# Second layer: half of the gated units as pairs of seven block products, with weight places taken in turn

## The chip, the cores and the metric

The kernel runs on one core of one Trainium2 chip. The metric is the device time of one execution in microseconds. Times given for a kernel are the median of several executions; a profile comes from one more execution, whose own time is given beside it.

## What is computed

One step of a two-layer decoder trunk for 512 prompt positions and 8 sample rows, which share all weights. The kernel treats them as one activation of 520 rows, held as 8 tiles of 128 channels x 520 columns. Only the second layer matters here:

```
def c_mixer(x, w_in, w_s, b_s, norm_v_g, norm_v_b, w_out):
    z = jnp.einsum('bld,de->ble', x, w_in)          # 1024 -> 3 x 2048
    u, v, g = jnp.split(z, (D_C, 2 * D_C), axis=-1)
    u = jax.nn.gelu(u)
    v = layer_norm(jax.nn.gelu(v), norm_v_g, norm_v_b)
    ...
    w_causal = w_s * jnp.tril(jnp.ones((CHUNK, CHUNK), w_s.dtype))
    mix = jnp.einsum('hts,bnshd->bnthd', w_causal, vc) + jnp.transpose(b_s)[None, None, :, :, None]
    ...
    y = u * mix * jax.nn.silu(g)
    return jnp.einsum('ble,ed->bld', y, w_out), v
...
xp = layer_norm(DEEPNORM_ALPHA * xp + out_p, ln_g[l], ln_b[l])
```

The first layer has the same shape: a wide input projection, two convolution branches, a gate, an output projection and a layer norm.

## The kernel before, in words

All matrix work is done in *units*: one unit is a 128-column slice of a weight matrix, 1024 x 128, which the host lays out as a tile of 128 x 8 x 128. There are 136 units; units 0 and 1 have a path of their own at the start. A unit is loaded as float32 (`raw_`), then split into a rounded part `whi_` (a cast on ACT) and the rest `wlo_` (a subtraction on DVE, or for 46 units of the first layer a copy on ACT and an accumulating DMA from POOL). The activations are split in the same way (`xh`, `xl`; `x1h`, `x1l` in the second layer; `yh`, `yl` for what enters an output projection). A product is then three matmuls for each of 8 k-tiles: high x high, low x high, high x low. `mm2` (line 161) does this for both halves of 260 columns, 48 matmuls a unit; `mm` (line 145) for one half, 24 matmuls. The results of a unit lie in a PSUM tile of two banks (`zt`, two such tiles); `cps` and `mps` give two single banks each.

`unit(n)` hands out unit n and loads units up to five ahead (`LEAD`). Weight tiles come from a common pool of 12 (tag W); units 70, 71, 134 and 135 take theirs from a pool M of 4. There are 3 raw tiles, 7 tiles for passing results (T), 4 more (B), and 8 + 8 long-lived tiles (AB and SB).

The code is written as a plain sequence; each instruction's place on its engine is set by a planner ahead of the run, which takes the earliest instruction in the code that can start by its estimated times, raised by `soon()` and lowered by `background()`. Each engine then runs its list strictly in that order and waits on semaphores.

The second layer runs in this order:

- 16 v units: GELU on ACT, then `v_tok` transposes the tile on PE (4 transposes of 128 x 128), copies it to a long-lived tile `vtok`, and takes its statistics on DVE. All 16 `vtok` tiles stay in the on-chip memory.
- `c_group(0)`: four u units (`z_u`, GELU), with `v_finish` after the first, which normalizes all 16 `vtok` tiles on DVE (line 658, 64 instructions). Then four gate units (`z_gc`, SiLU). `mix_unit` makes the mix of one unit from `vtok` (line 713, four matmuls) and `split_y` makes `yh` and `yl`. Then `c_group(4)` in the same way.
- eight output units over the first half of y (`z_q`); their results, with alpha times x1 added, stay in the on-chip memory as `r1`.
- `c_group(8)`, `c_group(12)`, and eight output units over the second half of y (`z_p`, by `out_part`, first columns 0 to 259, then the rest), with the final layer norm.

Of the kernel before, what the change touches and what calls it, by code (L numbers as in the profile page):

```python
# [16 lines left out]
P = 128  # L17
# [24 lines left out]

LEAD = 5
CUT = 260
# [5 lines left out]
def decoder_kernel(  # L50
# [35 lines left out]

    def ab_slot(name):
        return slots.tile([P, T], F32, tag="AB", name=name, bufs=8)

    def tmp(name):  # L90
        return tpool.tile([P, T], F32, tag="T", name=name, bufs=7)

# [18 lines left out]

    n_units = 2 + wu.shape[0]
    units = [None, None]

    def load_unit(wtag=("W", 12)):
        n = len(units)
        raw = wpool.tile([P, KT, P], F32, tag="raw", name=f"raw_{n}", bufs=3)
        nc.sync.dma_start(raw, wu[n - 2])
        hi = wpool.tile([P, KT, P], F32R, tag=wtag[0], name=f"whi_{n}", bufs=wtag[1])
        nc.scalar.copy(hi, raw)  # L120
        lo = wpool.tile([P, KT, P], F32R, tag=wtag[0], name=f"wlo_{n}", bufs=wtag[1])
        if n in BY_DMA:

            nc.scalar.mul(lo, raw, -1.0)  # L124
            nc.gpsimd.dma_start(lo, wu[n - 2], accum_op=ALU.add)  # L125
        else:
            nc.vector.tensor_tensor(lo, raw, hi.bitcast(F32), op=ALU.subtract)  # L127
        units.append((hi, lo))


    BY_DMA = set(range(10, 50)) | set(range(72, 78))
    EXTRA = set()
    for base in (64, 128):
        EXTRA.update((base + 6, base + 7))

    def unit(n):
        while len(units) < min(n + 1 + LEAD, n_units):
            load_unit(("M", 4) if len(units) in EXTRA else ("W", 12))
        return units[n]

# [14 lines left out]

    def mm2(z, w, ah, al):
        hi, lo = w
        for k in range(KT):
            for h in range(2):
                for j, (a, b) in enumerate(((hi, ah), (lo, ah), (hi, al))):  # L160
                    nc.tensor.matmul(  # L161
                        z[h][:, :TH],
                        a[:, k, :],
                        b[k][:, hs(h)],
                        start=(k == 0 and j == 0),
                        stop=(k == KT - 1 and j == 2),
                    )
# [15 lines left out]
    for k in range(KT):  # L183
        x = tmp(f"x_{k}")
        if k % 4 == 0:
            raw = wpool.tile([P, 4, 2, P], F32, tag="raw", name=f"raw_s{k}", bufs=3)
            w0h.append(wpool.tile([P, 4, 2, P], F32R, tag="W", name=f"whi_s{k}", bufs=12))
            w0l.append(wpool.tile([P, 4, 2, P], F32R, tag="W", name=f"wlo_s{k}", bufs=12))
        q, j = k // 4, k % 4
# [28 lines left out]

    load_unit()
    pa = const.tile([P, KT, NPA], F32, name="pa")  # L220
# [13 lines left out]


    unit(1)
    xs = []
    for j in range(2):
        t = wpool.tile([P, 4, NS, WA], F32, tag="M", name=f"xs_{j}", bufs=4)
        nc.sync.dma_start(t, cache_a[:, 4 * j : 4 * j + 4])  # L240
        xs.append(t)
# [45 lines left out]
    for i in range(KT):  # L287
# [24 lines left out]
        nc.gpsimd.dma_start(cap_out[:, i, :], ap[:, SEQ : SEQ + PADA])  # L312
        cA.append(ab_slot(f"cA_{i}"))
        if i % 2 == 1:
# [16 lines left out]
        nc.gpsimd.dma_start(cbp_out[:, i, :], ch[:, SEQ : SEQ + PADB])  # L331
        s = slots.tile([P, T], F32, tag="SB", name=f"sB_{i}", bufs=8)
        sB.append(s)
# [24 lines left out]
    with background():  # L358
        for j in range(2):
            nc.gpsimd.dma_start(cas_out[:, 4 * j : 4 * j + 4], xs[j])  # L360
            proda = wpool.tile([P, 4, NS, WA], F32, tag="M", name=f"proda_{j}", bufs=4)
# [95 lines left out]
    for d in range(KT):  # L457
        xr = tmp(f"xr_{d}")
        nc.sync.dma_start(xr, xT[:, d, :])
        r = slots.tile([P, T], F32, tag="SB", name=f"r_{d}", bufs=8)  # L460
        if d == 2:
# [15 lines left out]
    def out_part(base, c0, c1, yh, yl, res, lnc, done, last=False, pool_sub=()):  # L477
# [39 lines left out]
        def norm():  # L517
# [26 lines left out]
            for d in range(KT):  # L544
# [3 lines left out]
                if last:  # L548
                    if d % 4 == 0:
                        out = wpool.tile([P, 4, nn], F32, tag="raw", name=f"out_{d}", bufs=3)  # L550
                    o = out[:, d % 4, :]
# [39 lines left out]
    vs = tiny.tile([P, NV, NS], F32, name="vs")  # L591
    stats = wpool.tile([P, NC, NV, 6], F32, tag="M", name="stats", bufs=4)

    def v_tok(i):
        nc.gpsimd.tensor_copy(vs[:, i, :], vt[i][:, SEQ:])
        m = mt(f"vt_{i}")
        for c in range(NC):
            nc.tensor.transpose(m[:, c * P : (c + 1) * P], vt[i][:, c * P : (c + 1) * P], ident)  # L598
        t = ab_slot(f"vtok_{i}") if i < 8 else slots.tile([P, T], F32, tag="SB", name=f"vtok_{i}", bufs=8)
        nc.scalar.copy(t[:, :SEQ], m)  # L600
# [10 lines left out]
    for i in range(NVF):  # L611
# [6 lines left out]
        if i > 0:  # L618
            v_tok(i - 1)
    wt = wpool.tile([P, NH, P], F32, tag="M", name="wt", bufs=4)  # L620
    nc.gpsimd.dma_start(wt, wsT_in)
    bs = wpool.tile([P, NH, P], F32, tag="M", name="bs", bufs=4)
    nc.gpsimd.dma_start(bs, bs_in)
# [13 lines left out]
    for i in range(NVF, NV):  # L637
# [3 lines left out]
        nc.scalar.activation(two(vt[i]), zh(z), AF.Gelu_apprx_tanh)  # L641
        v_tok(i - 1)
    n += NV

    mv = tiny.tile([P, NC, 2], F32, name="mv")
    rs = tiny.tile([P, NC], F32, name="rs")
    mixs = tiny.tile([P, NV, NS], F32, name="mixs")
    rowsum = wpool.tile([P, NH, P], F32, tag="M", name="rowsum", bufs=4)

    def v_finish():  # L650
# [4 lines left out]
        nc.gpsimd.tensor_tensor(rs, rs, neg_half[:, :NC], op=ALU.pow)  # L655
        for i in range(NV):
            for c in range(NC):
                nc.vector.tensor_scalar(
                    vtok[i][:, c * P : (c + 1) * P],
                    vtok[i][:, c * P : (c + 1) * P],  # L660
                    mv[:, c, 0:1],
                    rs[:, c : c + 1],
                    op0=ALU.subtract,
                    op1=ALU.mult,
                )

# [37 lines left out]

    def mix_unit(i):
        h = i // 2
# [5 lines left out]
        for c in range(NC):  # L712
            nc.tensor.matmul(  # L713
                m[:, c * P : (c + 1) * P], vtok[i][:, c * P : (c + 1) * P], wt[:, h, :], start=True, stop=True
            )
# [10 lines left out]
        return t  # L726

    def c_group(g0):
        nonlocal n
        gu = []  # L730
        for i in range(g0, g0 + 4):
            z = zt(f"z_u{i}")
            mm2(halves(z), unit(n), x1h, x1l)
            n += 1
            t = btmp(f"gu_{i}")
            nc.scalar.activation(two(t), zh(z), AF.Gelu_apprx_tanh)
            gu.append(t)
            if i == 0:
                v_finish()

        def finish(i):
            t = gu[i - g0]
            split_y(i, t, mix_unit(i), "c", 1)

        for i in range(g0, g0 + 4):
            z = zt(f"z_gc{i}")
            mm2(halves(z), unit(n), x1h, x1l)
            n += 1
            g = tmp(f"silu_c{i}")
            t = gu[i - g0]  # L750
            nc.scalar.activation(two(g), zh(z), AF.Silu)
            nc.vector.tensor_tensor(t, g, t, op=ALU.mult)
            if g0 > 0:
                finish(i)
        if g0 == 0:
            for i in range(4):
                finish(i)

    yh, yl = [], []
    c_group(0)  # L760
    c_group(4)
    res = []
    for d in range(KT):
        z = zt(f"z_q{d}")
        mm2(halves(z), unit(n), yh, yl)
        n += 1
        r = ab_slot(f"r1_{d}")
        nc.vector.scalar_tensor_tensor(
# [3 lines left out]
            r, x1l[d].bitcast(F32), ALPHA, r, op0=ALU.mult, op1=ALU.add  # L772
        )
        res.append(r)
    yh, yl = [], []
    c_group(8)
    c_group(12)

# [108 lines left out]
```

## Time and profile before

| | |
|---|---|
| median of 3 executions | 826.85 us (826.73 to 828.02) |
| the profiled execution's own time | 827.27 us |
| its span, first to last instruction | 825.5 us |
| TensorE matmul busy | 811.8 us, 98% of the span |
| VectorE busy | 527.8 us, 64% |
| ScalarE busy | 351.9 us, 43% |
| GpSimd busy | 90.4 us, 11% |
| moved by DMA | 106.51 MB, 129 GB/s on average |

The times of the engines are busy times, and all engines run at once, so they do not add up. The page also cuts the span into 40 slices and gives each engine's busy share in each slice as a digit in tenths. Groups of instructions are listed by source line as "out<-in xcount | busy us, mean ns of one | idle time before". In the engines' names PE is TensorE, PEld its weight load, DVE VectorE, ACT ScalarE, POOL GpSimd and SP the engine that issues most loads. The v stage runs from about 458 to 520 us (its first part from 420), the gated stages from 520 to 620 and from 666 to 765.

### The profile page before, as it was taken

What the parts mean: (1) busy time and instruction counts of PE and PEld (TensorE: products, weight loads), DVE (VectorE), ACT (ScalarE), POOL (GpSimd) and SP (SyncE); (2) the same over time, 40 slices, a digit from 0 to 9 for tenths busy, and PEclk for the clock granted to TensorE, in tenths of its full rate; (3) what the DMA queues carried; (4) which work ended last, traced back from release to release, by engine and by line L of the source; (5) the groups of instructions that cost most, each with busy time, mean ns of one, the idle gap of its engine ahead of it and who ended that gap; (6) DMA issues with size and microseconds to landing.
All of it is one profiled execution on the core that took longest, in us unless ns stands there. A gap on an engine that the chain in (4) does not pass through costs nothing.

```text
span 825.5 us, 16037 instructions
## 1 busy us (share of the span) xinstructions
PE 811.8 (98%) x6792; PEld 809.9 (98%) x6792; DVE 527.8 (64%) x911; ACT 351.9 (43%) x515; POOL 90.4 (11%) x162
## 2 busy tenths in 40 slices
PE   8999999999999999999999999999999999999994
PEld 8999999999999999999999999999999999999994
DVE  5899998999963477355785423586255333626666
ACT  5544454444454445342668333333332133334243
POOL 0122221222111000000101411000000000000031
PEclk9999999999999999999999999999999999999997
DMA  8698988889878532322472422223322332232011
GB/s 301 203 205 185 215 182 186 184 187 223 180 172 198 180 115 77 104 88 92 113 195 91 163 80 78 77 83 101 100 79 78 102 82 98 77 97 84 1 53 53
DMA packets 33736, 106.51 MB, mean 129 GB/s; under 512 B 4304, under 2 KB 8032, under 8 KB 33664
## 3 DMA queue, kind: packets, MB, share of 16 engines
q1 hardware_dynamic: 26000, 79.01, 31.1%
q0 software_dynamic: 7664, 26.48, 17.0%
q8 instruction: 53, 0.87, 0.4%
q14 instruction: 19, 0.16, 0.1%
HBM read 102.03 MB, written 3.44 MB: 128 GB/s over the span
## 4 chain that ended last, share of the span: by engine, by line
PE 96%; DMA 1%; DVE 1%; ACT 1%; SPq 0%; issue 0%; ACTq 0%; DVEq 0%
PE z_p L145 11%; PE z_gc L161 11%; PE z_u L161 11%; PE z_v L161 7%; PE z_q L161 6%; PE z_o L161 6%; PE z_c L161 6%; PE z_ga L161 6%; PE z_post L161 6%; PE z_h L161 6%; PE z_gb L161 6%; PE z_val L161 5%; PE z_gate L161 5%; PE z_v L145 4%; PE mix L713 2%; PE vt L598 1%
## 5 line engine op out<-in xcount | busy, mean ns | idle before, releaser
L120 ACT CAST whi<-raw 128x1024 fp32r<-128x1024 f32 x134 | 139.9, 1048 | 322.8 <-PE z_u L161 44.9
L127 DVE TENSOR_TENSOR wlo<-raw,whi 128x1024 fp32r<-128x1024 f32 x88 | 107.4, 1225 | 140.5 <-ACT whi L120 140.5
L273 DVE SCALAR_TENSOR_TENSOR acc<-apad,pa,acc 128x512 f32<-128x512 f32 x240 | 165.6, 750 | 3.6 <-ACT acc L270 2.7
L161 PE MATMUL z_gc<-x1h,whi 128*128 128x260 f32 x256 | 72.9, 285 | 0.0
L161 PE MATMUL z_u<-x1h,whi 128*128 128x260 f32 x256 | 72.4, 283 | 0.0
L125 POOL DMA_DIRECT2D wlo<-in_wu x46 | 40.1, 871 | 292.7 <-ACT msq L529 140.3
L161 PE MATMUL z_gc<-x1h,wlo 128*128 128x260 f32 x256 | 72.0, 281 | 0.0
L161 PE MATMUL z_u<-x1l,whi 128*128 128x260 f32 x256 | 72.0, 281 | 0.0
L161 PE MATMUL z_gc<-x1l,whi 128*128 128x260 f32 x256 | 72.0, 281 | 0.0
L161 PE MATMUL z_u<-x1h,wlo 128*128 128x260 f32 x256 | 72.0, 281 | 0.0
L124 ACT ACTIVATE wlo<-raw 128x1024 fp32r<-128x1024 f32 x46 | 48.5, 1055 | 0.0
L161 PEld LDWEIGHTS z_u<-x1h,wlo 128*128 128x128 f32 x256 | 48.1, 188 | 0.1
L161 PEld LDWEIGHTS z_gc<-x1h,wlo 128*128 128x128 f32 x256 | 48.2, 188 | 0.0
L161 PEld LDWEIGHTS z_u<-x1h,whi 128*128 128x128 f32 x256 | 48.1, 188 | 0.1
L161 PEld LDWEIGHTS z_u<-x1l,whi 128*128 128x128 f32 x256 | 48.1, 188 | 0.0
L161 PEld LDWEIGHTS z_gc<-x1l,whi 128*128 128x128 f32 x256 | 48.1, 188 | 0.0
L161 PEld LDWEIGHTS z_gc<-x1h,whi 128*128 128x128 f32 x256 | 48.1, 188 | 0.0
L161 PE MATMUL z_v<-x1h,whi 128*128 128x260 f32 x160 | 46.0, 288 | 0.0
L161 PE MATMUL z_v<-x1l,whi 128*128 128x260 f32 x160 | 45.0, 281 | 0.0
L161 PE MATMUL z_v<-x1h,wlo 128*128 128x260 f32 x160 | 45.0, 281 | 0.0
L161 PE MATMUL z_c<-xh,wlo 128*128 128x260 f32 x128 | 36.1, 282 | 0.3 <-DVE wlo L127 0.3
L145 PE MATMUL z_p<-yh_c,whi 128*128 128x260 f32 x128 | 36.3, 285 | 0.0
(258 smaller groups left out, 2706.0 us busy)
## 6 DMA issues: line engine op xcount, KB each, us to landing
raw<-in_wu SPq DMA_DIRECT2D x134, 512.0 KB, 4.0
wlo<-in_wu POOLq DMA_DIRECT2D x46, 512.0 KB, 7.9
xr<-in_xT SPq DMA_DIRECT2D x8, 260.0 KB, 4.6
x<-in_xT SPq DMA_DIRECT2D x7, 260.0 KB, 4.7
out_y<-r SPq DMA_DIRECT2D x8, 130.0 KB, 1.7
out_y<-out SPq DMA_DIRECT2D x4, 260.0 KB, 2.4
raw_s<-in_w SPq DMA_DIRECT2D x8, 128.0 KB, 4.4
xs<-in_cache_a SPq DMA_DIRECT2D x2, 496.0 KB, 8.5
```

Source lines behind the costliest of these rows:

```text
L120: nc.scalar.copy(hi, raw)
L124: nc.scalar.mul(lo, raw, -1.0)
L125: nc.gpsimd.dma_start(lo, wu[n - 2], accum_op=ALU.add)
L127: nc.vector.tensor_tensor(lo, raw, hi.bitcast(F32), op=ALU.subtract)
L145: nc.tensor.matmul(ps, a[:, k, :], b[k][:, c], start=(k == 0 and j == 0), stop=(k == KT - 1 and j == 2),)
L161: nc.tensor.matmul(z[h][:, :TH], a[:, k, :], b[k][:, hs(h)], start=(k == 0 and j == 0), stop=(k == KT - 1 and j == 2),)
L273: nc.vector.scalar_tensor_tensor(acc[i], apads[i][:, j : j + SEQ], pa[:, i, PA_W + j : PA_W + j + 1], acc[i], op0=ALU.mult, op1=ALU.add,)
L598: nc.tensor.transpose(m[:, c * P : (c + 1) * P], vt[i][:, c * P : (c + 1) * P], ident)
L713: nc.tensor.matmul(m[:, c * P : (c + 1) * P], vtok[i][:, c * P : (c + 1) * P], wt[:, h, :], start=True, stop=True)
```

## The change

In each four of u units and each four of gate units (there are eight fours), the first two units are computed as a pair, as a 2 x 2 block product in the Winograd form of Strassen's scheme. The weight blocks are the two units by the two halves of the 1024 inputs; the activation blocks are the two halves of inputs by the two halves of 260 columns. Seven products of four k-tiles replace eight.

- `load_pair` makes the weight forms of a pair: a11 and a12 (unit 1 as it is), a22, s1, s3, s2 and s4, with four additions on DVE, and each form split into a high and a low part. That is seven weight tiles of full size for a pair.
- `x_forms` makes the four activation forms, during the v units 6, 8, 10 and 12: for each of four k, eight DVE instructions and four casts on ACT, with 260 columns each.
- `Seven` runs the products in the order p1, p5, p2, p6, p7, p4, p3. They accumulate in two PSUM banks (p2 has a third); ACT copies out an intermediate sum and DVE adds others in the on-chip memory. The function then runs on the sum there, not out of PSUM.
- `c_four` puts the third unit of the four between the products: p1, p5, p2, p6, half of unit 3, p7, the other half, p4, p3, then unit 4.
- Weight tiles come from six places of two tiles each, taken in turn; a pair takes four places. Units are loaded ahead until ten tiles are ahead (five single units). The casts of the weights from unit 88 on, and the functions of the fours, are each kept in code order on ACT.
- To make room, each `vtok` tile is stored to memory by a DMA from POOL and fetched again by SP for its mix, with normalizing then (half of it on DVE, half on ACT) in place of line 658; the eight `r1` tiles are stored and fetched too. T has 5 tiles instead of 7, M 3 instead of 4, raw 4 instead of 3.
- In a gate four, the last step of each output (`finish`) comes when its function has run: for the pair and the third unit this is after p3.

```
-LEAD = 5
+RING = 6
+NRAW = 4
+AHEAD = 10
...
+    spill = ctx.enter_context(tc.tile_pool(name="spill", bufs=1, space=bass.MemoryType.DRAM))
...
-        return tpool.tile([P, T], F32, tag="T", name=name, bufs=7)
+        return tpool.tile([P, T], F32, tag="T", name=name, bufs=5)
...
+    def load_pair(n1, n2):
+        r1, r2 = load_raw(n1), load_raw(n2)
+        a1 = parts(n1, r1)
+        a22 = w_slot(f"wa22_{n1}", place_of(), (P, 2, 4, P))
+        high(a22[:, 0], r2[:, 4:], n2)
+        nc.vector.tensor_tensor(a22[:, 1], r2[:, 4:], a22[:, 0].bitcast(F32), op=ALU.subtract)
+        nc.vector.tensor_tensor(r2[:, :4], r2[:, :4], r2[:, 4:], op=ALU.add)
+        nc.vector.tensor_tensor(r1[:, :4], r1[:, :4], r2[:, :4], op=ALU.add)
+        nc.vector.tensor_tensor(r2[:, 4:], r1[:, :4], r2[:, 4:], op=ALU.subtract)
+        s13 = parts(n2, r2, kind="s")
+        nc.vector.tensor_tensor(r1[:, 4:], r1[:, 4:], r1[:, :4], op=ALU.add)
+        s24 = parts(n1, r1, kind="s")
...
+    def need(*job):
+        j = place[job]
+        ahead = lambda: sum(2 if len(q) == 1 else 7 for q in JOBS[j + 1 : len(loaded)])
+        while len(loaded) < len(JOBS) and (len(loaded) <= j or ahead() < AHEAD):
+            q = JOBS[len(loaded)]
+            loaded.append(load_unit(*q) if len(q) == 1 else load_pair(*q))
+        return loaded[j]
...
-        vtok[i] = t
+        vtok[i] = spill.tile([P, SEQ], F32, name=f"vd_{i}")
+        nc.gpsimd.dma_start(vtok[i], t)
...
+        def p1(self):
+            self.w = need(*self.job)
+            z = zt(f"z_{self.key}")
+            self.b1, self.b2 = z[:, 0, :TH], z[:, 1, :TH]
+            product(self.b1, self.w["a11"], self.x(0, 0), True)
+            self.copy(self.c1[:, hs(0)], self.b1)
+        def p5(self):
+            product(self.b2, self.w["s1"], self.f(1), True)
+        def p2(self):
+            b3 = cps.tile([P, SEQ], F32, tag="cv", name=f"z_{self.key}_2")[:, :TH]
+            product(b3, self.w["a12"], self.x(1, 0), True)
+            self.add(self.c1[:, hs(0)], b3)
+        def p6(self):
+            product(self.b1, self.w["s2"], self.f(2))
+            self.copy(self.c1[:, hs(1)], self.b1)
+        def p7(self):
+            product(self.b1, self.w["s3"], self.f(3))
+            self.copy(self.c2[:, hs(1)], self.b1)
+            self.add(self.c2[:, hs(1)], self.b2)
+        def p4(self):
+            product(self.b1, self.w["a22"], self.f(4))
+            self.copy(self.c2[:, hs(0)], self.b1)
+        def p3(self):
+            product(self.b2, self.w["s4"], self.x(1, 1))
+            self.add(self.c1[:, hs(1)], self.b2)
...
+    def fetch(i):
+        t = tpool.tile([P, SEQ], F32, tag="V", name=f"vback_{i}", bufs=2)
+        nc.sync.dma_start(t, vtok[i])
...
+        flight[:] = [Seven(f"{tag}{m}", (m, m + 1), ts[0], ts[1]).steps(), ends]
+        stop()
+        z = zt(f"z_{tag}{m + 2}")
+        w = unit(m + 2)
+        mm2(halves(z), w, x1h, x1l, range(KT // 2))
+        stop()
+        mm2(halves(z), w, x1h, x1l, range(KT // 2, KT))
+        with soon():
+            nc.scalar.copy(two(ts[2]), zh(z))
+        stop(True)
+        apply(2)
+        z = zt(f"z_{tag}{m + 3}")
+        mm2(halves(z), unit(m + 3), x1h, x1l)
+        apply(3, zh(z))
...
+        for e in range(g0, g0 + 4):
+            back[e] = fetch(e)
+        c_four(m + 4, "g", tmp, AF.Silu, lambda j, g: finish(g0 + j, us[j], g))
```

More of the change, by code (lines that the diff above doesn't have):

```diff
@@ L109, in hs, with place_of, w_slot, load_raw @@
         return slice(h * TH, (h + 1) * TH)
[L112 to L117, printed above, removed]
-        nc.sync.dma_start(raw, wu[n - 2])
[L119 to L122, printed above, removed]
+    turn = [0]
+    def place_of():
+        turn[0] += 1
+        return f"W{turn[0] % RING}"
+    def w_slot(name, tag, shape=(P, KT, P)):
+        return wpool.tile(list(shape), F32R, tag=tag, name=name, bufs={"M": 3, "raw": NRAW}.get(tag, 2))
+    def load_raw(n):
+        raw = wpool.tile([P, KT, P], F32, tag="raw", name=f"raw_{n}", bufs=NRAW)
+        nc.sync.dma_start(raw, wu[n - 2])
+        return raw
+    class Chain:
+        def __init__(self):
+            self.last = None
+        def add(self, make):
+            if self.last is None:
+                self.last = make().ins
+            else:
+                with tc.issue_after(self.last):
+                    ins = make().ins
+                self.last = ins
+    casts = Chain()
+    def high(out, src, n):
+        if n >= 88:
+            casts.add(lambda: nc.scalar.copy(out, src))
+        else:
+            nc.scalar.copy(out, src)
+    def parts(n, raw, tags=None, kind="w"):
+        tags = tags or [place_of()] * 2
+        hi = w_slot(f"{kind}hi_{n}", tags[0])
+        high(hi, raw, n)
+        lo = w_slot(f"{kind}lo_{n}", tags[1])
+        if n in BY_DMA and kind == "w":
             nc.scalar.mul(lo, raw, -1.0)
@@ L549, in norm @@
                     if d % 4 == 0:
[L550 removed]
+                        out = wpool.tile([P, 4, nn], F32, tag="raw", name=f"out_{d}", bufs=NRAW)
                     o = out[:, d % 4, :]
@@ new lines, in product, with __init__, x, f @@
+    def product(ps, a, b, first=False):
+        for k in range(4):
+            (ah, al), (bh, bl) = a(k), b(k)
+            for j, (p, q) in enumerate(((ah, bh), (al, bh), (ah, bl))):
+                nc.tensor.matmul(
+                    ps, p, q, start=(first and k == 0 and j == 0), stop=(k == 3 and j == 2),
+                    skip_group_check=True,
+                )
+    class Seven:
+        def __init__(self, key, job, c1, c2):
+            self.key, self.job, self.c1, self.c2 = key, job, c1, c2
+        def x(self, half, h):
+            return lambda k: (x1h[4 * half + k][:, hs(h)], x1l[4 * half + k][:, hs(h)])
+        def f(self, j):
+            return lambda k: (xf[j - 1][k][:, 0], xf[j - 1][k][:, 1])
+        def copy(self, out, src):
+            with soon():
+                nc.scalar.copy(out, src)
+        def add(self, out, src):
+            with soon():
+                nc.vector.tensor_tensor(out, out, src, op=ALU.add)
+        def p1(self):
[23 more added lines that the diff above has]
+            self.add(self.c1[:, hs(1)], self.b2)
+        def steps(self):
+            self.p1()
+            self.p5()
+            self.p2()
+            self.p6()
+            yield
+            self.p7()
+            yield
+            self.p4()
+            self.p3()
@@ L642, in decoder_kernel @@
         v_tok(i - 1)
+        if i % 2 == 0 and i < NVF + 8:
+            x_forms((i - NVF) // 2)
     n += NV
@@ L726, in mix_unit @@
         return t
-    def c_group(g0):
[L729 to L754, printed above, removed]
-        if g0 == 0:
-            for i in range(4):
-                finish(i)
+    back = {}
@@ new lines, in finish, with stop, c_four, apply @@
+    def finish(i, u, g):
+        nc.vector.tensor_tensor(u, u, g, op=ALU.mult)
+        split_y(i, u, mix_unit(i, back[i]), "c", 1)
+    funcs = Chain()
+    flight = [iter(()), lambda: None]
+    def stop(last=False):
+        for _ in flight[0]:
+            if not last:
+                return
+        then, flight[1] = flight[1], lambda: None
+        then()
+    def c_four(m, tag, out, func, done):
+        ts = [out(f"{tag}_{m + j}") for j in range(4)]
+        def apply(j, src=None, sign=1.0):
+            t = ts[j]
+            if src is None:
+                funcs.add(lambda: nc.scalar.activation(t, t, func, scale=sign))
+            else:
+                funcs.add(lambda: nc.scalar.activation(two(t), src, func))
+            done(j, t)
+        def ends():
+            apply(0)
+            apply(1, sign=-1.0)
+        flight[:] = [Seven(f"{tag}{m}", (m, m + 1), ts[0], ts[1]).steps(), ends]
[5 more added lines that the diff above has]
+        mm2(halves(z), w, x1h, x1l, range(KT // 2, KT))
+        with soon():
+            nc.scalar.copy(two(ts[2]), zh(z))
[4 more added lines that the diff above has]
+        apply(3, zh(z))
```

146 lines of the change are left out of this document (98 added, 48 removed).

## The prediction

> **What bounds the kernel now.** I read the page first: span, busy shares, slices, and the shares of the chain that ended last.
>
> ```profile
> span 825.5 us, 16037 instructions
> PE 811.8 (98%) x6792; PEld 809.9 (98%) x6792; DVE 527.8 (64%) x911; ACT 351.9 (43%) x515; POOL 90.4 (11%) x162
> PE   8999999999999999999999999999999999999994
> DVE  5899998999963477355785423586255333626666
> ACT  5544454444454445342668333333332133334243
> PEclk9999999999999999999999999999999999999997
> PE 96%; DMA 1%; DVE 1%; ACT 1%; SPq 0%; issue 0%; ACTq 0%; DVEq 0%
> ```
>
> TensorE (PE) is busy in every slice but the first and the last, at the full granted clock, and is 96% of the chain. A busy PE could still hide waits, so the waits of PE come next, all of them:
>
> ```profile
> PE warm L174 <- DVE warm L171: 1.1, 1, 1.1
> PE z_first L211 <- ACT xh L204: 0.8, 1, 0.8
> PE z_c L161 <- DVE wlo L127: 0.3, 1, 0.3
> ```
>
> They sum to 2.2 us, all at the start. So an instruction taken off PE shortens the run by PE's pitch, as long as nothing new makes PE wait. The pitch is in the chain in order of time (start, us, what, count):
>
> ```profile
> 619.97 46.06 PE z_q L161 x384
> 666.03 22.85 PE z_u L161 x192
> 688.88 5.70 PE z_gc L161 x48
> 695.47 5.73 PE z_gc L161 x48
> 764.72 14.96 PE z_p L145 x125
> ```
>
> 22.85 / 192 = 119.0 ns from one 260-column matmul to the next (a unit of 48 is 5.71 us). Between two z_gc units lie 695.47 − 688.88 − 5.70 = 0.89 us, the four mix matmuls. Then the other engines by stage, since the change works only where u and z_gc are made (520 to 620 and 666 to 765) and in the v stage ahead of it (458 to 520):
>
> ```profile
> core 0: us, PE busy (x) PEld busy (x) DVE busy (x) ACT busy (x) POOL busy (x), PEclk, DMA share, GB/s
> 15.00:189.00 174.00, 173.72 (x1461) 173.52 (x1461) 160.76 (x233) 84.93 (x104) 36.06 (x59) 1.00 0.87 202
> 373.00:458.00 85.00, 85.00 (x710) 84.88 (x709) 56.02 (x138) 52.11 (x102) 11.09 (x14) 1.00 0.45 128
> 458.00:520.00 62.00, 62.00 (x525) 62.00 (x524) 21.11 (x55) 21.08 (x32) 11.52 (x15) 1.00 0.32 95
> 520.00:620.00 100.00, 100.00 (x842) 99.83 (x842) 62.20 (x141) 35.28 (x48) 5.99 (x14) 1.00 0.27 86
> 666.00:689.00 23.00, 23.00 (x196) 23.00 (x195) 6.21 (x6) 7.24 (x9) 0.00 (x0) 1.00 0.30 94
> 689.00:715.00 26.00, 26.00 (x222) 26.00 (x222) 13.51 (x19) 9.88 (x13) 0.75 (x3) 1.00 0.24 82
> 805.00:825.50 20.50, 8.99 (x68) 8.33 (x67) 13.99 (x35) 7.27 (x17) 3.49 (x5) 0.79 0.16 53
> ```
>
> There PE is full, while VectorE (DVE) has 19.7 us of work in a group's 49 us (666 to 715) and ScalarE (ACT) 17.1: room for the additions the change asks of them.
>
> **The change part by part.** Durations of the operations it uses (x count | busy, mean ns | idle):
>
> ```profile
> L120 ACT CAST whi<-raw 128x1024 fp32r<-128x1024 f32 x134 | 139.9, 1048 | 322.8 <-PE z_u L161 44.9 <-PE z_v L161 40.5 <-PE z_q L161 34.5
> L127 DVE TENSOR_TENSOR wlo<-raw,whi 128x1024 fp32r<-128x1024 f32 x88 | 107.4, 1225 | 140.5 <-ACT whi L120 140.5
> L658 DVE TENSOR_SCALAR vtok<-vtok,mv,rs 128x128 f32<-128x128 f32 x64 | 16.5, 347 | 0.4 <-POOL rs L655 0.4
> L491 DVE TENSOR_TENSOR r<-z_p,r 128x260 f32<-128x260 f32 x32 | 13.0, 422 | 12.7 <-PE z_p L145 12.7
> L717 DVE SCALAR_TENSOR_TENSOR mix<-mix,pv,cm 128x512 f32<-128x512 f32 x16 | 12.0, 749 | 29.2 <-PE mix L713 29.2
> L406 DVE TENSOR_TENSOR yl_c<-gu,yh_c 128x520 fp32r<-128x520 f32 x16 | 11.2, 699 | 11.0 <-ACT yh_c L405 11.0
> L752 DVE TENSOR_TENSOR gu<-silu_c,gu 128x520 f32<-128x520 f32 x16 | 11.1, 696 | 0.3
> L404 DVE TENSOR_TENSOR gu<-gu,mix 128x520 f32<-128x520 f32 x16 | 11.1, 694 | 0.2
> L405 ACT CAST yh_c<-gu 128x520 fp32r<-128x520 f32 x16 | 10.0, 627 | 34.8 <-DVE gu L404 34.8
> L736 ACT ACTIVATE gu<-z_u 128x520 f32<-128x520 f32 x16 | 9.6, 601 | 9.4 <-PE z_u L161 9.4
> L708 DVE SCALAR_TENSOR_TENSOR cm<-rowsum,pv,bs 128x128 f32<-128x128 f32 x16 | 5.5, 341 | 0.0
> L751 ACT ACT_TABLE_LOAD x4 | 5.1, 1283 | 0.1
> L610 ACT COPY v<-z_v 128x260 f32<-128x260 f32 x6 | 2.2, 370 | 4.2 <-PE z_v L145 4.2
> ```
>
> *Matmuls.* Two units are 2 x 48 = 96 matmuls; seven products of 4 k-tiles x 3 are 84, with the same 128x128 weights and 260 columns. Eight pairs: 8 x 12 = 96 fewer, 96 x 119.0 ns = **−11.42 us**. No matmul is added: transposes and mix stay. A rule to hold against this: in the Trainium skill's page "TensorE: Matmul & The Clock Gate", section "Wait — 56ns, not 53.3ns?", a warm matmul starts every N / 2.4 GHz plus about 2.5 ns, 110.8 ns for 260 columns, which would make the term 10.64 us. The row says 119.0, and the row is used.
>
> *Handing over PSUM inside a pair.* This wait is new: p6, p7 and p4 write the bank that ACT must first have copied, p3 the one that DVE must have added. Between an emptied product and the next in its bank lie 24 other matmuls (2.86 us; p3: 36, 4.28 us). An ACT copy is 0.37, with one cast ahead of it (1.05) 1.42 us: hidden. The bad case is cast, table load and function first, 1.05 + 1.28 + 0.60 + 0.37 = 3.30, 0.44 late; tables change about once per four, so 8 x 0.44 = 3.5 us is the upper end and 0 the lower (a gain is excluded, PE has no idle to give back here). Nearest row: 373 to 458, where half units of 24 matmuls are emptied by the same engines at some 65% busy, and PE is busy 85.00 of 85 us, though over more banks. I take **+1.0**, near the lower end. If the cover goes, all later matmuls of the four queue behind the waiting one.
>
> *Weight forms.* DVE per pair: three subtractions of 1024 columns (3.68), one of 512 (at most 0.70), four additions of 512 (2.80): 7.2 us where two units had 2.45. Plus three adds from PSUM (1.27) and the two plain units (2.45): 10.9 us per four, against 180 x 0.119 = 21.4 us of PE. A gate four also finishes four outputs, 4 x (0.696 + 0.694 + 0.749 + 0.341 + 0.699) = 12.7, and normalizes four fetched tiles, 8 x 0.347 = 2.8: 26.4 us in 21.4 + 4 x 0.89 = 25.0. The u and gate four together: 37.3 of 46.4 us, 80%. (Means overstate: the group at 666 to 715 would sum to 22.5 by them and shows 19.7.) ACT: 6 casts less one half, four copies, one more copy of a full tile, four functions, half of the normalizing, four casts of y: below 60%. So both fit on average, and the gate four's surplus of 1.4 us is prefetch that can slide. The form due soonest is s24: its place frees after p3, it is needed at the next p6, 48 + 36 matmuls = 10.0 us later; cast and subtraction take 2.3. Cost 0. Without that cover it is 2.3 us per four.
>
> *Six places in turn, raw 4, M 3, T 5.* Still 12 weight tiles, and five units ahead for single units as before. A four uses exactly six places, so a pair's successor waits only for s24 as above. SP is passed by 24 more loads (16 v tiles, 8 residuals), POOL by 24 stores. T from 7 to 5 in the first layer: its reuse is one or two tiles per 5.7 us unit. Cost 0; bounds ±0.5, from the 0.3 + 0.8 us of start waits that one more raw tile can touch.
>
> *v tiles and residual through memory.* 16 x 256 KB and 8 x 260 KB out and back, 12.5 MB over 245 us: 51 GB/s on top of 86, where the first stage carries 202.
>
> ```profile
> raw<-in_wu SPq DMA_DIRECT2D x134, 512.0 KB, 4.0
> wlo<-in_wu POOLq DMA_DIRECT2D x46, 512.0 KB, 7.9
> ```
>
> A store of half that size holds its T tile under 7.9 us, so two of five at one unit per 6.2 us; x_forms takes two for some 4 us: four of five. x_forms on DVE: 4 x 8 x 0.42 = 13.5 us on top of 21.11 in 62 us. The 64 normalizations that ran in one block (16.5 us) are gone from v_finish. All beside PE: 0.
>
> *The ends of the halves.* Silu of three gate units now waits for p3, so four outputs finish together. After p3: silu 0.60, then three chains on DVE of 3 x 3.2 = 9.5 us, then the last unit's. PE meanwhile has m+3 and mix (5.71 + 3.56 = 9.3), then 42 matmuls of z_q (5.0 us) ahead of the last y. The last chain ends about 9.3 + 0.6 + 3.2 + 0.6 = 13.7, cover 14.3. In z_p the cover is shorter, but there, before the change, the last yl_c is this late already:
>
> ```profile
> 769.97 0.70 DVE L406 TENSOR_TENSOR yl_c<-gu,yh_c 128x520 fp32r<-128x520 f32 x1 [0.75 <-ACT yh_c L405]
> ```
>
> It ends 5.9 us after z_p began at 764.72, while 21 matmuls reach the last k in 2.5 us, and PE ran 14.96 us without a wait: it took up later tiles first. Bounds 0 to 2 x 1.5; I take **+0.5**.
>
> **Sum.** The profiled execution took 827.27 us (span 825.5 and 1.8 around it). 827.27 − 11.42 + 1.0 + 0.5 = 817.35. The median shown, 826.85, lies 0.42 lower: **816.9 us**. With every end: 814.9 (no new waits, −0.5) to 822.4 (+3.5 + 3.0 + 0.5); likely 815 to 819.5.
>
> **Rivals.**
> *The fetched v tiles come late.* Two slots: the third fetch starts when the first mix has left PE, lands 4.0 us later, and is normalized in about 1.4. That is 5.4 against 5.71 + 1.78 = 7.5 us of PE work. Behind one weight load on SP (4.0) it is 9.4, about 2 us late, and with its finish some 2.8 at each half's end, where all eight outputs are wanted: +5.6, 822.5. For it: the queue is in order. Against: DMA is at 0.27 share here. Chance 0.10.
> *Slower: the handovers cost what the matmuls gave.* One mechanism: PE waits at p6, p7, p4 and p3 of each four, 32 times, because the copy stands behind ACT or DVE work that itself waits. It decides at 11.42 / 32 = 0.36 us each; at 0.5 us it is +16, 831.4. For it: gate fours load DVE to its limit, and ACT and DVE take instructions in their order. Against: the 2.86 us of cover, and the 85 us without a wait above. Chance 0.09.
> *Slower: stores from POOL held up by DVE.* If a v store kept its T tile over 3 x 6.2 = 18.5 us, v_tok's copy would wait on ACT, the next GELU behind it, and PE for PSUM: at 25 us, 25/3 − 6.2 = 2.1 us in each of 10 units, +21, 836. Against: POOL's transfers landed in 7.9 us where DVE was 92% busy (160.76 of 174). Chance 0.03. By the Trainium skill's page "SBUF — State Buffer", section "Who interferes with whom", DVE operations with two SBUF inputs or in a two-port mode and POOL share a port pair as an exclusive lock. By that rule stores could starve; the trace's 7.9 us shows that they did not.
> *No change.* The losses above, each half grown, sum to 10 to 13 us: within 1.65 us of 826.85. Chance 0.04.
>
> **How the numbers follow.** My forecast has 0.74. A measurement of this kernel tells from no change what is over about 0.2% (1.65 us). Faster: 0.74 + 0.10 = 0.84; same 0.04; slower 0.12. 815 to 822.5 holds the first two; I widen by about 0.5 for the unknown start: 814.6 to 823.
>
> **What would show it.** Right: 6696 PE instructions; PE waits in the gated stages under 2 us in all; a u four about 21.4 us; DVE near 70 to 80% there; v stage still 62 us. Handover: PE waits on ACT copies or DVE adds of the pair's own tiles. Late forms: PE waits on wlo, slo or a22. Fetch: PE waits on vback or yl_c at z_q and z_p. POOL: v units longer than 6.2 us. The forecast is wrong if PE's sum of waits passes 3 us, or if the first layer grows.

## The result: 882.89 us, 6.7% slower than before

The changed kernel took a median of 882.89 us (881.17 to 884.34, 4 runs) beside 826.82 for the kernel before on the same chip: ratio 1.0674, 95% interval 1.0649 to 1.0699. The profiled execution took 881.17 us, its span is 879.5. The prediction was 816.9 us, with a range up to 823. It was wrong by its sign and by 66 us.

Span, busy shares, slices and the shares of the chain that ended last, on the page of the kernel after:

```profile
span 879.5 us, 16193 instructions
PE 823.0 (94%) x6696; PEld 816.2 (93%) x6696; DVE 571.5 (65%) x984; ACT 395.0 (45%) x619; POOL 112.7 (13%) x186
...
PE   9999999999999999999999999976989988779794
...
PEclk9999999999999999999999999989999989879998
...
PE 89%; ACT 6%; DVE 1%; DMA 1%; issue 1%; SPq 0%; ACTq 0%; DVEq 0%
```

The 96 matmuls are gone (6792 to 6696), yet PE is busy longer, and both PE rows have holes from the 27th slice on. ACT, 1% of the chain before, is 6% of it. The view of waits on PE, from its top:

```profile
PE z_g L245 <- ACT u L948: 12.5, 4, 4.1
PE z_g L717 <- ACT whi L149: 9.1, 2, 4.6
PE z_u L245 <- ACT u L963: 6.2, 2, 3.1
PE z_p L229 <- ACT g L948: 5.3, 1, 5.3
PE z_q L245 <- ACT g L948: 3.1, 1, 3.1
PE z_u L245 <- ACT g L948: 1.6, 2, 1.2
```

(Columns: us in total, times, longest.) From the first u matmul on they are 22 waits of 43.1 us, and none of them is a wait of p6, p7, p4 or p3 (L717 here is p1 or p2). 22.5 us end with L948, the function of the *fourth* unit of a four; the 9.1 us end with a weight cast that stands in the same queue of ACT. The chain that ended last shows one of them (start, us, what, count):

```profile
734.73 2.75 PE z_g L245 x23
737.47 1.43 PE z_g L717 x12
738.90 2.86 PE z_g L245 x24
741.76 1.33 PE z_g L717 x11
...
744.06 1.99 ACT whi L149 x2
...
746.07 1.28 ACT L946
...
747.36 1.69 ACT g L946 x3
749.05 0.93 ACT whi L149
...
751.06 7.65 PE z_u L245 x48
```

L245 here is unit 4, L717 at 737.47 is p4 and at 741.76 p3. PE's list is not the code's: unit 4 runs *around* p4 and p3 instead of after them. So when p3 ends nothing of the four is left to cover what follows. PE has p1 of the next u four (12 matmuls, up to 745.5 us), then in its list one matmul of the gate four after that, whose `whi` ACT casts only behind the three functions, then unit 3 of the u four. The three functions wait for p3's sum and a table load; the fourth (L948) stands behind them and behind casts, and it alone frees the PSUM tile that unit 3 needs. After the gap the unit of 48 takes 7.65 us instead of 5.71. The view by stretches of time shows the clock there:

```profile
736.00:744.00 8.00, 7.53 (x63) 7.32 (x62) 1.63 (x5) 2.91 (x6) 0.00 (x0) 1.00 0.34 101
744.00:752.00 8.00, 3.00 (x17) 2.50 (x17) 7.46 (x10) 7.61 (x11) 1.13 (x2) 0.74 0.59 197
752.00:759.00 7.00, 7.00 (x50) 7.00 (x49) 7.00 (x13) 1.63 (x3) 0.60 (x1) 0.80 0.01 2
```

(Columns: stretch, its length; busy and count of PE, PEld, DVE, ACT, POOL; granted clock, DMA share, GB/s.)

By stage, from the first u matmul to the first of z_q, to the last of z_q, to the last gate matmul, to PE's end, with the sum of PE's waits in brackets:

| | first half | z_q | second half | rest | sum |
|---|---|---|---|---|---|
| before | 100.5 (0) | 46.1 (0) | 97.7 (0) | 49.8 (0) | 294.1 |
| after | 118.6 (15.3) | 52.4 (4.1) | 121.6 (17.4) | 56.0 (6.3) | 348.6 |
| chain | 107.3 (7.1) | 49.3 (0.9) | 106.8 (6.8) | 50.0 (2.8) | 313.4 |
| line | 103.1 (4.5) | 46.1 (0) | 102.7 (4.8) | 46.5 (0.2) | 298.4 |
| apart_only | 97.9 (2.2) | 47.9 (0) | 96.3 (2.4) | 49.1 (0.2) | 291.2 |
| apart | 95.2 (0) | 46.1 (0) | 93.9 (0) | 48.2 (0) | 283.4 |

u starts at 518.8 us after and at 519.2 before: the first layer and the v stage cost nothing. After loses 54.5 us and the 11.4 that seven products save, 65.9 in all. Of this 43.1 are the 22 waits of PE, some 6 the pipeline that each of them drains (0.26 us, see *line*), and by difference some 17 the lower clock. The trace's record of the clock agrees: it is at half for 44.4 us from the first u matmul on, PE is busy for 35.7 of them, and half of that is 17.8.

### The profile page after: what moved, and what is told of

Same layout as the page of the kernel before. It is cut to its first block, busy times and chain, and to the rows that moved or that the text cites. A ratio compares the mean times of both kernels' runs of the same rounds, so it can differ in the third digit from the quotient of the medians.

```text
span 879.5 us, 16193 instructions
## 1 busy us (share of the span) xinstructions
PE 823.0 (94%) x6696; PEld 816.2 (93%) x6696; DVE 571.5 (65%) x984; ACT 395.0 (45%) x619; POOL 112.7 (13%) x186
## 4 chain that ended last, share of the span: by engine, by line
PE 89%; ACT 6%; DVE 1%; DMA 1%; issue 1%; SPq 0%; ACTq 0%; DVEq 0%
PE z_p L229 10%; PE z_v L245 7%; PE z_u L245 6%; PE z_g L245 6%; PE z_o L245 5%; PE z_gb L245 5%; PE z_c L245 5%; PE z_ga L245 5%; PE z_h L245 5%; PE z_post L245 5%; PE z_gate L245 5%; PE z_val L245 5%; PE z_q L245 4%; PE z_v L229 4%; PE z_u L717 4%; PE z_g L717 4%
## 5 line engine op out<-in xcount | busy, mean ns | idle before, releaser
L149 ACT CAST whi<-raw 128x1024 fp32r<-128x1024 f32 x40 | 40.7, 1043 | 44.1 <-PE z_q L245 15.3
L245 PE MATMUL z_g<-x1h,whi 128*128 128x260 f32 x128 | 39.9, 312 | 12.5 <-ACT u L948 12.5
L245 PE MATMUL z_u<-x1h,whi 128*128 128x260 f32 x128 | 40.5, 316 | 7.8 <-ACT u L963 6.2
L245 PE MATMUL z_v<-x1h,whi 128*128 128x260 f32 x160 | 46.0, 287 | 0.0
L245 PE MATMUL z_v<-x1l,whi 128*128 128x260 f32 x160 | 45.1, 282 | 0.0
L245 PE MATMUL z_v<-x1h,wlo 128*128 128x260 f32 x160 | 45.0, 281 | 0.0
L245 PE MATMUL z_q<-yh_c,whi 128*128 128x260 f32 x128 | 36.5, 286 | 3.9 <-ACT g L948 3.1
L245 PE MATMUL z_u<-x1h,wlo 128*128 128x260 f32 x128 | 39.5, 309 | 0.0
L245 PE MATMUL z_u<-x1l,whi 128*128 128x260 f32 x128 | 39.4, 308 | 0.0
L245 PEld LDWEIGHTS z_g<-x1h,whi 128*128 128x128 f32 x128 | 27.0, 211 | 13.3 <-ACT u L948 13.2
L245 PE MATMUL z_g<-x1h,wlo 128*128 128x260 f32 x128 | 38.9, 304 | 0.0
L245 PE MATMUL z_g<-x1l,whi 128*128 128x260 f32 x128 | 38.8, 303 | 0.0
L229 PE MATMUL z_p<-yl_c,whi 128*128 128x260 f32 x128 | 35.9, 288 | 0.9 <-DVE yl_c L491 0.9
L163 DVE TENSOR_TENSOR slo<-raw,shi 128x1024 fp32r<-128x1024 f32 x16 | 19.6, 1224 | 26.3 <-ACT shi L149 26.3
```

The source lines that it names most:

```text
L149: casts.add(lambda: nc.scalar.copy(out, src))
L229: nc.tensor.matmul(ps, a[:, k, :], b[k][:, c], start=(k == 0 and j == 0), stop=(k == KT - 1 and j == 2),)
L245: nc.tensor.matmul(z[h][:, :TH], a[:, k, :], b[k][:, hs(h)], start=(k == 0 and j == 0), stop=(k == KT - 1 and j == 2),)
```

## The experiments

All ratios are to the kernel before, with 95% intervals.

**plain: everything but the pairs.** All four units of a four go through `mm2`; `x_forms` is not issued; places, tile counts, stores and fetches are the change's.

```
-        flight[:] = [Seven(...).steps(), ends]   ... p1 to p3, unit 3, unit 4
+        for j in range(4):
+            z = zt(f"z_{tag}{m + j}")
+            mm2(halves(z), unit(m + j), x1h, x1l)
+            apply(j, zh(z))
```

> All of the change except the pairs: each four is four plain units (768 matmuls in the gated stages as before), no activation forms, no block products; v tiles and residual go through memory, six weight places, raw 4, M 3, T 5 stay. If the loss comes from the pairs (theory), this is the kernel before: 825 to 830 us, PE waits under 3 us. If the moves through memory, the five T tiles or the places cost (rival), it is 835 to 880, with PE or ACT waits on vback, vd or T tiles.

827.18 us, 0.9998 [0.9989, 1.0008], no wait of PE in the gated stages. The weight places and the v tiles through memory cost nothing; the loss is in the pairs.

**free4, order4, nofuncs, vdve: who holds unit 4's tile.** free4 copies unit 4 out of PSUM at once; order4 holds unit 4's matmuls behind p3 on PE; nofuncs takes the functions off their chain; vdve normalizes the fetched tiles on DVE alone.

```
free4:   -        apply(3, zh(z))
         +        with soon():
         +            nc.scalar.copy(two(ts[3]), zh(z))
         +        apply(3)
order4:  ...   (last_mm[0] is the pair's last matmul so far, here p3's)
         -        mm2(halves(z), unit(m + 3), x1h, x1l)
         +        w = unit(m + 3)
         +        with tc.issue_after(last_mm[0]):
         +            mm2(halves(z), w, x1h, x1l)
nofuncs: ...   (the same for the function on a sum)
         -  funcs.add(lambda: nc.scalar.activation(two(t), src, func))
         +  nc.scalar.activation(two(t), src, func)
vdve:    -  if c < 2: nc.vector.tensor_scalar(b, b, ...)   else: nc.scalar.activation(b, b, ...)
         +  nc.vector.tensor_scalar(b, b, ...)
```

> The fourth unit of each four is copied out of PSUM at once, as the third is, and its function runs on the copy. Theory (the fourth function, last of its chain behind p3, three functions, three casts and a table load, holds the PSUM tile that the next four needs): the 22.5 us of PE waits on line 948 go and part of the half-clock matmuls after them, 845 to 860 us. Rival (the weight casts or the DMA of the v tiles are late by themselves): PE waits as long for whi, shi or vback, 875 to 885 us.

> The 48 matmuls of the fourth unit are kept behind p3 on PE, the order that the prediction worked with. Theory: p3, the three functions and the casts then run under 5.7 us of matmuls and the waits on line 948 shrink to below 1.5 us per four; new waits at p4 and p3 for the copies appear, 0.5 to 1 us each; in all 845 to 865 us. Rival (ACT has too much to do at this place whatever PE's order): 875 us or more.

> The changed kernel with the functions of a four free to stand in any order on ACT. Theory (the planner's order on PE is the cause, the chain of functions one link of it): the fourth function can run before p3 and the 22.5 us of waits on line 948 mostly go, but the waits on whi and on the fetch stay; 855 to 872 us, like the copy that freed unit 4's PSUM (869.4). Rival (the chain of functions does nothing): 880 to 885 us.

> The fetched v tiles are normalized on DVE alone, so that ACT never stands waiting for a fetch. If ACT, blocked by the fetch, holds the third unit's copy (theory, a second and smaller loss): the 6.2 us of PE waits on line 963 go, with some slow matmuls: 868 to 878 us. If the fetch is not what the copy waits for (rival): no change, 881 to 886 us.

free4 869.36 us, 1.0507 [1.0486, 1.0528]; order4 844.28, 1.0204 [1.0175, 1.0232]; nofuncs 857.93, 1.0363 [1.0330, 1.0395]; vdve 876.8, 1.0597 [1.0576, 1.0618]. Each removes a part: the release of unit 4 by a late function is real (nofuncs 25 us), more goes with unit 4's place (order4 39 us), and taking ACT off the fetched tiles is worth 6 us. free4 missed its range: unit 4's copy came late too, and PE still waited 11.4 us for it. But order4 still lost 17 us, in waits that had not been there:

```profile
590.99 1.71 PE L719 MATMUL z_u<-xf,wa 128*128 128x260 f32 x12 [2.61 <-DVE u L743]
...
593.16 0.39 PE L719 MATMUL z_u<-x1h,shi 128*128 128x260 f32 x1 [0.46 <-ACT u L739]
...
618.81 0.39 PE L719 MATMUL z_g<-x1h,shi 128*128 128x260 f32 x1 [2.09 <-ACT g L739]
```

The second and third are p3, which writes bank b2, waiting for ACT's copy of p4, which reads bank b1. The first is p4, which writes b1, waiting for a DVE addition. I did not read these rows rightly at this point.

**chain, chain_vdve, early: order and the late finish.** chain puts all matmuls of the fours on PE in the code's order; early multiplies the mix into u ahead of the gate four, so that `finish` is only the last product and the split.

```
chain: -  nc.tensor.matmul(ps, p, q, ...)
       +  line.add(lambda: nc.tensor.matmul(ps, p, q, ...))       # line = Chain(), also in mm2
early: -  nc.vector.tensor_tensor(u, u, g, op=ALU.mult)
       -  split_y(i, u, mix_unit(i, back[i]), "c", 1)
       +  split_y(i, u, g, "c", 1)
       ...
       -  back[e] = fetch(e)
       +  nc.vector.tensor_tensor(us[e - g0], us[e - g0], mix_unit(e, fetch(e)), op=ALU.mult)
```

> All matmuls of the fours stand on PE in the order of the code: p1, p5, p2, p6, half of unit 3, p7, half, p4, p3, unit 4. Theory (the loss comes from the order that the planner gave PE, which took away the matmuls that were to cover the copies and the functions): each handover has its 2.86 us and the functions their 5.7 us again, PE waits in the gated stages fall below 10 us, 820 to 832 us. Rival (ACT and DVE cannot keep up with the pairs in whatever order): PE waits remain at 20 us or more, 840 to 850 us, as with unit 4 alone held back (844.3).

> The code's order on PE, and the fetched v tiles normalized on DVE alone. If ACT, waiting in its line for a fetch, is what remains: 2 to 6 us below the code's order alone. If DVE's load in the gate fours is what remains (rival): 2 us or more above it, since DVE gets 8 more instructions of 0.35 us per gate four.

> The changed kernel with the mix multiplied into u ahead of the gate four, so that after p3 only u times silu, the cast and the subtraction are left (2.1 instead of 3.2 us of DVE per output, and no wait for a fetch there). PE's order is left to the planner. Theory (PE's order and the functions' chain are the larger part, the crowd on DVE behind p3 the smaller): 860 to 876 us. Rival (the crowd on DVE is the main cause): below 850 us.

chain 846.1 us, 1.0215 [1.0193, 1.0237], no better than order4: the theory that order was all fell. PE still waited 7.4 us at mixes and 6.4 us for the pairs' copies. chain_vdve 840.57, 1.0153 [1.0123, 1.0183]; early 874.63, 1.0574 [1.0553, 1.0595]. Early mixes alone leave the order's loss in place.

**chain_early and its variants.** Both at once, then with vdve, then with four of the additions for the weight forms on POOL.

> The code's order on PE and the mix multiplied in early. Theory now (with the order mended, what remains of 846.1 us is the crowd on DVE behind p3, which keeps PSUM from the mix and the copies of the next four): 818 to 832 us. Rival (what remains is ACT, with casts, table load and functions behind p3): 838 to 846 us, with PE waits on ACT copies.

> As the run before, and the fetched v tiles normalized on DVE alone. If ACT's place in the fetch still costs: 2 to 6 us below the run before; if DVE is now the nearer limit: the same or above.

> As the run before, and the four additions of each pair's weight forms on POOL, which is idle there. If DVE's load is what remains: 2 to 5 us below the run before, at 816 to 826 us. If not (rival): within 2 us, or above where the sums come later.

830.48 us, 1.0038 [1.0024, 1.0052]; 832.69, 1.0070 [1.0051, 1.0089]; 831.8, 1.0048 [1.0032, 1.0065]. Order and finish together are worth 52 us. Shifting work from ACT to DVE or from DVE to POOL no longer helps: neither engine as a whole is what PE waits for.

**line, line_vdve.** As chain_early, with the four mixes of a gate four spread over that four, in PE's order too.

> All PE work of the fours in the code's order, the mixes too, and these spread over the gate four (behind p6, half of unit 3, the other half, and p3), with the fetch of the third and fourth tile behind the first two mixes. Theory (in the kernel with early mixes, at 830.5 us, the rest of the loss is PE standing at a mix that the planner had put ahead of its inputs, 5 us, with 3 to 4 us of slow clock behind): 818 to 826 us, faster than before. Rival (the pairs' own handovers and the weight forms cost as much as the 96 matmuls give): 826 us or more.

> As the run before, with the fetched tiles normalized on DVE alone. ACT is then never behind a fetch, but DVE has 2.8 us more per gate four. If DVE's load there is near its limit (theory): 1 to 4 us above the run before; if ACT's place matters more: below it.

831.71 us, 1.0050 [1.0036, 1.0064], and 831.88, 1.0057 [1.0044, 1.0071]. Both missed what their theories said, but what is left in line has a pattern:

```profile
PE z_u L724 <- ACT u L746: 6.0, 7, 1.9
PE z_g L724 <- ACT g L746: 3.3, 7, 0.5
```

Nearly every p5 waits for the copy of p1, and nearly every p3 for the copy of p4. One p5 in the timeline of line, with the last matmul of p1, the copy and the first matmuls of p5:

```profile
544.88 0.28 PE L724 MATMUL z_g<-x1l,whi 128*128 128x260 f32 x1
...
545.20 0.38 ACT L746 COPY g<-z_g 128x260 f32<-128x260 f32 x1
...
545.62 0.39 PE L724 MATMUL z_g<-xf,shi 128*128 128x260 f32 x1 [0.47 <-ACT g L746]
...
545.85 0.28 PE L724 MATMUL z_g<-xf,slo 128*128 128x260 f32 x1
```

p5 does not read or write what the copy reads; it writes the other bank of the same PSUM tile. Here ACT is not late at all (0.04 us after p1's end), and PE still waits. From 544.88 to 545.85 are 0.97 us for two pitches (0.24): the handover costs about 0.73, not 0.47. Matmuls overlap (each lasts 0.28 us and the next starts after 0.12), so 0.16 us more is lost while the last one ends alone, and the first one after the wait takes 0.39: the pipeline drains and fills again, for 0.26 us.

**apart, swap, apart_early: the tile.** apart is line with p5 and p3 in a PSUM tile of their own; swap leaves the tile and covers the copies by order (p1, p2, p5, p6, three eighths of unit 3, p7, three eighths, p4, two eighths, p3); apart_early is chain_early with the tile parted.

```
-            self.b1, self.b2 = z[:, 0, :TH], z[:, 1, :TH]
+            self.b1 = z[:, 0, :TH]
+            self.b2 = cps.tile([P, SEQ], F32, tag="cv", name=f"z_{self.key}_3")[:, :TH]
```

> As line, but the product of p5 and p3 has a PSUM tile of its own (a single bank of the two that p2 takes in turn) in place of the second bank of the pair's tile. Theory (a tile of two banks is one thing to a wait: PE may not write its second bank while ACT copies the first): line waited 0.47 us in each of 8 p5 for the copy of p1, 0.47 in each of 8 p3 for the copy of p4, and 1.4 more in two of the p5; these 16 waits go, and with p5 and p2 (2.86 us) behind p1 the two long ones go too. 831.7 - 16 x 0.47 - 2 x 1.4 = 821.4; 819 to 824. Rival (the waits are ACT's being late, and the next product that needs the bank itself, p6, waits in their place; or DVE is the limit): 828 to 832.

> As line, in another order: p1, p2, p5, p6, three eighths of unit 3, p7, three eighths, p4, two eighths, p3, unit 4; the banks as in the change. p2 lies in its own bank between p1 and p5, and 12 matmuls of unit 3 between p4 and p3 (1.43 us each). Theory (p5 and p3 only lacked cover for an ACT copy of 0.37 us): the 16 waits of 0.47 us go, the two of 1.89 us shrink to 0.5; but p7 and p4 have 18 and 12 matmuls of cover instead of 24, and the copy of unit 3 comes 12 matmuls later, so some waits of some tenths come back: 821 to 826. Rival (ACT or DVE as a whole is late): 828 to 832.

> As chain_early (the four matmul groups in code order, the mixes free, each mix multiplied into u ahead of its gate four), with p5 and p3 in a PSUM tile of their own. chain_early waited 1.9 + 1.4 us for ACT copies and functions and some 7 us at mixes. Theory: the first go, 830.5 - 16 x 0.47 = 823; 821 to 826, and it stands beside apart by what the place of the mixes costs. Rival: no change, 829 to 831.

apart 817.19 us (816.89 to 818.50), 0.9880 [0.9867, 0.9893]; swap 832.98, 1.0068 [1.0054, 1.0083]; apart_early 822.61, 0.9945 [0.9932, 0.9958]. In apart these are all the waits PE has, at the start as in the kernel before, and the stretches of the gated stages are full at full clock:

```profile
PE warm L262 <- DVE warm L259: 1.1, 1, 1.1
PE z_c L245 <- DVE wlo L163: 0.4, 1, 0.4
```

```profile
519.00:615.00 96.00, 96.00 (x806) 95.83 (x806) 68.40 (x126) 54.72 (x90) 13.37 (x14) 1.00 0.39 123
661.00:755.00 94.00, 94.00 (x793) 94.00 (x792) 62.27 (x95) 52.25 (x82) 7.53 (x9) 1.00 0.44 142
```

DVE (68.40 of 96 us) and ACT (54.72) have room. The gain over line, 14.5 us, answers to the 14 waits shown of it: 9.3 us, 14 x 0.26 = 3.6 of draining, and 1.7 for the 3.41 us at half clock behind one of them. apart_early has its mixes early but not spread, and lies 5.4 us above apart. swap's miss shows the same tile from its other side:

```profile
558.88 1.71 PE L724 MATMUL z_g<-xf,wa 128*128 128x260 f32 x12 [1.34 <-DVE g L750]
...
576.22 0.49 PE L724 MATMUL z_u<-xf,shi 128*128 128x260 f32 x1 [2.39 <-ACT u L746]
```

p4 writes b1 and waits for the addition of p7, which reads b2; and a p5 waits 2.39 us for a copy of p1 that stood behind casts on ACT, more than one product can cover. Cover by order does not stretch over a whole tile's readers.

**apart_only, apart_chain: the tile alone.** apart_only is the change with that one edit; apart_chain adds the order.

> The change with one edit: the product of p5 and p3 has a PSUM tile of its own (as in apart); nothing is put in code order by hand and finish is as in the change. Theory A (the tile of two banks, waited for as one, is the cause of all that the change lost: of the waits, and of the planner's putting unit 4 ahead of p3): no wait for a function or for the copies of the pair is left, the mixes cost no more than in before, where they stood in the same place: 816 to 822. Theory B (the late finish, with its mixes and chain of functions, has a price of its own once a four is quick, as chain against chain_early showed 15.6 us): 825 to 835.

> apart_only with the matmul groups of the fours held in code order on PE (chain with p5 and p3 in a tile of their own). Against apart_only it shows what the planner's order still costs once the tile is parted. Theory A: the same within 2 us (816 to 822). Theory B: 825 to 835 as apart_only. A third case, that the order itself costs: apart_chain below apart_only by 3 us or more.

apart_only 824.05 us, 0.9967 [0.9954, 0.9980]; apart_chain 819.54, 0.9907 [0.9893, 0.9921]. apart_only lies between the two theories' ranges, 2 us above A's and 1 us below B's, and apart_chain in the third case, 4.5 us below it. One PSUM tile more takes 58.8 us off the change. PE's order is almost the code's now, without a chain: unit 4 follows p3, but for 4 to 18 of its 48 matmuls in three of the eight fours. So the shared tile had also shaped the order; that the planner filled the waits it foresaw at p4 and p3 with unit 4 is the likely reason, and is not shown. The edit also lets the pair's first tile go after p4's copy instead of p3's addition; no run parts the two, but in line and apart 48 matmuls of unit 4 lie between p3 and the next p1, so there the 14.5 us are the waits. What is left over apart_chain is 4.5 us, with these waits:

```profile
PE z_g L717 <- ACT shi L149: 4.3, 2, 2.4
PE z_u L717 <- ACT u L737: 0.3, 1, 0.3
```

```profile
584.46 0.39 PE L717 MATMUL z_g<-xf,shi 128*128 128x260 f32 x1 [1.92 <-ACT shi L149]
```

A single p5 matmul of the next gate four stands in PE's list ahead of p4 of the u four and waits for its weight cast. apart_chain in turn has two waits in the gated stages, both of p6 for ACT's copy of p1, which stands behind casts. This is the wait that the prediction named, at 2.1 us:

```profile
PE z_u L724 <- ACT u L746: 2.1, 2, 1.2
```

```profile
574.37 0.39 PE L724 MATMUL z_u<-xf,shi 128*128 128x260 f32 x1 [1.23 <-ACT u L746]
```

Mixes multiplied in early and spread over the gate four give the last 2.4 us (819.54 to 817.19); multiplied in early but not spread they cost 3.1 instead (apart_early, 822.61).

So the 65.7 us from 882.89 to 817.19 are 58.8 for the tile, 4.5 for the planner's order, 2.4 for mixes spread ahead of the finish. The Trainium skill's page "Perfetto Trace Analysis", section "Matmuls", says that independent groups should rotate through different banks so that emptying one overlaps the next group. Here different banks alone did not give that overlap (line, 831.71 us); banks in different tiles did (apart, 817.19).

## Why the prediction was wrong, step by step

- *Matmuls* (−11.42): right. 6696 PE instructions; in apart, where nothing waits, the stages sum to 283.4 us against 294.1, 10.7 less.
- *Handing over PSUM inside a pair* (+1.0, upper end +3.5): **the step that failed.** It listed p6, p7, p4 and p3 by the bank that each writes, with 24 or 36 matmuls of cover. The kernel waits by the tile: p5 for the copy of p1 and p3 for the copy of p4, with no product between, and p4 for the addition of p7's b2 (rows of line, order4 and swap). It also took the code's order for PE's: in the change itself the planner had put other matmuls in those places, and PE waited elsewhere, for unit 4's late function above all. Measured, the term is 58.8 us in the change (apart_only), 26.6 with PE held to the code's order (chain against apart_chain), and 14.5 with the mixes put right too (line against apart). No unit of the kernel before has a tile that one engine reads by one bank while another writes its second, so the row taken as nearest (373 to 458) did not hold this case, and the upper end of 3.5 had no bound for it. An estimate from the prediction's own rows, 16 handovers without cover at an ACT copy of 0.37 us, would have given 6 us. Where each bank has its own tile the term was right: 2.1 us in apart_chain, 0 in apart.
- *Weight forms* (0): right on the average, wrong in place. DVE is 71% busy in apart's first half, within the 70 to 80% named, and no wait there is for a form. In the change the forms' casts stand in the same queue as the functions; `whi` (9.1 us) and in apart_only `shi` (4.3 us) appear as releasers when PE's list asks for a pair too early.
- *Six places, raw 4, M 3, T 5* and *v tiles and residual through memory* (0): right; plain has both, though no pairs, and took 827.18 us, and in apart PE waits for neither. vd stores landed in 4.7 us and fetches in 2.8 (medians). The normalizing half on ACT cost 6 us in the change (vdve) and nothing in line.
- *x_forms* (hidden): right. DVE's 33.40 us of the 61 from 458 to 519, against 20.10 in plain: 13.3 for the 13.5 worked out; PE full.
- *The ends of the halves* (+0.5): wrong in the change (3.1 and 5.3 us at z_q and z_p, for L948). With the tile parted (apart_only) z_q takes 1.8 us longer than before and the rest 0.7 less: +1.1.
- *Rivals.* "Handovers cost what the matmuls gave" (0.09) had the kind of wait, and its 831.4 us is what line and chain_early measured, but at p5 and p3 rather than at p6, p7, p4 and p3, and for a reason it did not have. None had the reordering or the clock. POOL's stores were not it (z_v units unchanged). The late fetch was a small part: some 6 us through ACT's queue in the change (vdve) and in chain (chain_vdve), 2.2 us at one mix of chain_early, nothing in line and apart.

The sum itself (817.35 for the profiled execution) is near what the change takes once its PSUM tile, its order and its mixes are altered: apart's profiled execution took 816.89 us. That is another kernel than the one predicted, and the closeness is partly chance: it gains 10.7 us in the stages where the sum has 11.42, and has none of the 1.5 us of waits that the sum allows.

## What to carry to other kernels

In this kernel a wait belonged to a tile, not to a bank. So list, for every write into a tile, each reader of *any* part of it that is still at work, and ask what runs on the engine between them. Where two accumulators have different lives, give them different tiles. A forced wait can also move the order in which a planner puts the rest, so look at the engine's real order before pricing any cover; here the tile cost 58.8 us with the planner's order and 26.6 with the code's.

## What the runs showed of the hardware

A short wait of PE costs more than the trace's number: 0.47 us of idle time made the next product about 0.73 us late (rows of line above).

PE's clock can fall after a wait. In the timeline of after, the matmuls from 718.92 follow a wait of 4.12 us, those from 643.75 one of 3.14; the clock is the third number from the end, 0.50 and 1.00:

```profile
718.90:724.00 5.10, 5.08 (x23) 5.08 (x24) 4.53 (x8) 1.70 (x3) 0.00 (x0) 0.50 0.43 146
643.70:650.00 6.30, 6.25 (x53) 6.25 (x54) 6.30 (x12) 1.88 (x3) 0.57 (x1) 1.00 0.31 111
```

In line a wait of 1.89 us was followed by 0.61 at 573.6 to 578, and another of 1.89 by 1.00 at 721.8 to 726. The Trainium skill's page "TensorE: Matmul & The Clock Gate", section "HAM oscillation — how this bites in real kernels", puts the bite at gaps over about 3.4 us. These rows show it after shorter ones, and not after each.

The traces show what decides. In the 20 traces the granted clock changes only at whole steps of 3.41 us from one another. Here are four such steps of line, two around each wait of 1.89 us (the first number behind the length is PE's busy time):

```profile
570.61:574.02 3.41, 1.52 (x13) 1.32 (x12) 3.41 (x5) 2.95 (x6) 3.40 (x1) 1.00 0.37 133
574.02:577.43 3.41, 3.41 (x18) 3.41 (x18) 1.94 (x4) 0.63 (x1) 2.00 (x1) 0.50 0.53 154
717.38:720.79 3.41, 2.60 (x22) 2.40 (x21) 3.41 (x8) 3.41 (x7) 2.16 (x2) 1.00 0.68 215
720.79:724.20 3.41, 2.33 (x19) 2.33 (x20) 3.41 (x5) 1.66 (x4) 3.41 (x1) 1.00 0.40 106
```

The first wait lies inside one step, PE is busy for 45% of it (1.52 of 3.41), and the next step has half the clock. The second wait is parted by the end of a step, PE is busy for 76% and 68%, and the clock stays. So it is in after: 3.14 us parted over two steps (57% and 51% busy) cost no clock, 4.12 us with 30% in one step did. Over all traces, from 20 us into the run to PE's last matmul, the clock halved after each of the 42 steps at full clock in which PE was busy 45% or less, and after none with 60% or more; in between it did either.
